# Elementwise work of norm rows, scans and combinations moved from GpSimd to VectorE in a four-layer mixed-attention forward pass

## The chip, the cores and the metric

One Trainium2 chip, one of its cores. The time is the device time of one execution of the whole forward pass in microseconds. The engines of the core are TensorE (PE in the profile; its weight loads are PEld), VectorE (DVE), ScalarE (ACT), GpSimd (POOL) and SyncE (SP, which issues most DMA transfers). Each executes its own list of instructions in order and waits for the others by semaphores.

## The reference

512 latent tokens and 256 context tokens, 1024 channels. Two blocks of two layers follow each other. In the first block, each layer is a norm with modulation by a condition (a gain and an offset per channel, different for latent and context tokens), two mixers side by side, a projection, a second such norm and an MLP. Layer 0 mixes by differential attention and a recurrent delta rule; layer 1 by two scans that run forwards and backwards, a state space scan (SSD, in chunks of 128) and a gated linear attention (GLA, here worked out in levels of halving blocks).

```python
def rmsnorm(x, g, eps=EPS):
    y = xf * lax.rsqrt(jnp.mean(xf * xf, axis=-1, keepdims=True) + eps)
    return (y * g.astype(F32)).astype(x.dtype)
...
        h = rmsnorm_2(x, norm1[l])
        proj = h @ w_in[l]
        o_a = dilated_mixture(...)
        o_b = stick_breaking_attention(...)
        merged = g_a * (o_a @ w_br[l, :OUT_A]) + g_b * (o_b @ w_br[l, OUT_A:])
        x = x + merged @ w_o[l]
        h2 = rmsnorm_2(x, norm2[l])
        up = h2 @ w_up[l]
        a = causal_depthwise_conv(a, conv_w[l], conv_b[l])
        x = x + (jax.nn.gelu(a, approximate=False) * v) @ w_down[l]
```

The second part of this is a layer of the second block: a mixture of windowed attentions of three dilations, each with its own softmax, that are combined by their maxima and denominators; a stick-breaking attention with a running sum of log-sigmoids; gates, projection, norm, and a gated MLP with a short convolution.

## The kernel before, in words

Channels lie on the 128 partitions and tokens along the free axis. Every large product is done in three passes of reduced-precision float32: an operand is split in a high half, which is its rounded copy, and a low half, which is what the rounding left; high by high, high by low and low by high are summed in PSUM. So each strip of weights (128 x 1024) that a DMA brings (`raw`, two buffers) goes through `_split` (L525): ScalarE casts it to `whi`, and then `wlo` = `raw` - `whi` is taken. By default VectorE takes it; while the flag `lazy` is set, GpSimd does. `layer1` sets the flag around the run of its mixers (L1748 to L1750).

The order of the work is made by a planner in the kernel (`Plan`, cost table at L300, `run` at L403). Stages are written as generators. `run` advances the one whose inputs are ready soonest by the planner's own costs of each engine; generators of the lowest priority (`FILL`) yield columns of a projection and go where nothing else is ready. Each instruction is recorded as it is yielded, and its order on its engine is fixed from then on. A changed engine of an instruction changes these costs and so the order of later instructions. All instructions go through one recording method (`Lane.call`, L245), so the profile tells them by the tiles that they write and read, not by lines.

What the change touches:

- `ada` (L768): the norm rows. For each of 8 channel groups, VectorE multiplies a piece by 1/rms (`t`), ScalarE makes the high half `H` of gain * t + offset, GpSimd makes the same in full (`u`, a `t` in the profile, L783), and VectorE subtracts. It runs at the second norm of layer 0 (two pieces of 384 tokens, 846 to 893 us), at the first norm of layer 1 (pieces of 512 and 256, up to 1463 us) and at the second norm of layer 1 (two pieces of 256, 1827 to 1857 us): 56 scalings.
- Layer 1's mixers (1446 to 1790 us). `layer1` (L1584) runs `fill()` (columns of the input projection, at the end the GLA's part of the output projection), `second()` (the GLA) and `first()` (the SSD). In `ssd_mix` (L1808) a step transposes decays into PSUM, ScalarE takes the exponential `E`, GpSimd multiplies it by C (`cT`, L1836), VectorE adds a mask (`G<-m,neg`), ScalarE takes the exponential of each head and VectorE multiplies by dt and C.B (`G<-G,sdt,cb`). In `gla_levels` (L1906) a level makes factors `QF` and `KF` from differences of cumulated decays (VectorE), their exponentials (ScalarE) and products with q and k (L1950, L1951; GpSimd for QF, and for KF of odd head pairs). `gla_prep` (L1896) has two differences on GpSimd, `gla_carry` (L2007) the product `qe`, `gla_post` (L2085) the output gate `yg` * `gs`. The convolution of the SSD (`t<-t,cw,t`, `bb`) is on VectorE in the same stretch.
- `block2` (L2141): in `dil` (L2355, L2359) the denominators' products and sums of the three dilations, once for each half of the heads and each layer; in `sb` (L2415) the running sums.

```python
        self.nc.scalar.copy(hi, raw)
        (self.nc.gpsimd if self.lazy else self.nc.vector).tensor_tensor(lo, raw, hi.bitcast(F32), op=SUB)
...
            nc.gpsimd.tensor_tensor(QF, QF, qT[:, t, :], op=MUL)
            (nc.gpsimd if t else nc.vector).tensor_tensor(KF, KF, kl[:, t, :], op=MUL)
```

## Time and profile before

| | before |
|---|---|
| median of 3 runs (lowest to highest) | 3707.17 us (3707.15 to 3709.8) |
| profiled execution, its span | 3708.26 us, 3706.5 us |
| mean granted TensorE clock | 0.983 |
| busy: PE, PEld | 3533.2 us (95%), 2935.0 us (79%) |
| busy: DVE, ACT, POOL | 2088.9 us (56%), 1540.0 us (42%), 641.9 us (17%) |
| instructions: PE, DVE, ACT, POOL | 25118, 3733, 2992, 817 |

Busy time is a mean over stages whose limits differ; the stretches are told apart by cutting the span into windows. The engine names in the rows are PE, PEld, DVE, ACT, POOL and SP. In a row of instructions, `out<-in` names the tile written and those read, then come partitions x elements and types of both, the count, busy time, mean time of one in ns, and the idle time of the engine before them with what ended it. Buffer numbers are left out, so several tiles share a name.

### The profile page before, as it was taken

To read this page: it belongs to the slowest core of one execution; us is meant where nothing else is said; L and a number is where in the kernel's file an instruction comes from. 1 tells how busy PE (TensorE), PEld (TensorE's weight loads), DVE (VectorE), ACT (ScalarE), POOL (GpSimd) and SP (SyncE) were. 2 spreads that over 40 slices of the span, in tenths; PEclk is the share of its full clock that TensorE was granted. 3 is DMA by queue.
4 is the path that set the end of the run, shared out by engine and by line. 5 is a ranking of instruction groups with operands and counts; after the bars stand their busy time and mean duration, and the time that the engine had idled before them with its cause. 6 is when DMAs were issued, how large, how long until landed. Compare 5 with 4: busy or idle time off the path is not lost.

```text
span 3706.5 us, 61484 instructions
## 1 busy us (share of the span) xinstructions
PE 3533.2 (95%) x25118; PEld 2935.0 (79%) x25118; DVE 2088.9 (56%) x3733; ACT 1540.0 (42%) x2992; POOL 641.9 (17%) x817
## 2 busy tenths in 40 slices
PE   7998998999999998888899999999999999999998
PEld 5786787888999997776788877777888777778886
DVE  5636787865433346588654465655554356555542
ACT  5424666634212224344532244555333245544331
POOL 3314233202000002443300020003110000031100
PEclk9999999999999999989999999999999999999999
DMA  5423311123333312110222232223333322232332
GB/s 207 114 82 130 126 50 38 32 89 114 109 125 111 117 63 88 52 41 24 97 96 97 98 120 71 63 74 109 97 97 101 124 68 63 74 103 94 97 95 90
DMA packets 128346, 337.10 MB, mean 91 GB/s; under 512 B 41536, under 2 KB 44608, under 8 KB 126912
## 3 DMA queue, kind: packets, MB, share of 16 engines
q1 hardware_dynamic: 113168, 297.31, 25.1%
q10 hardware_dynamic: 12432, 27.47, 2.3%
q0 software_dynamic: 2464, 8.39, 0.6%
q8 instruction: 198, 3.24, 0.4%
q14 instruction: 84, 0.69, 0.1%
HBM read 315.30 MB, written 17.83 MB: 90 GB/s over the span
## 4 chain that ended last, share of the span: by engine, by line
PE 67%; DVE 8%; ACT 2%; POOL 1%; issue 1%; DVEq 0%; POOLq 0%; ACTq 0%
PE g L245 61%; PE m L245 6%; DVE t L245 3%; POOL t L245 1%; DVE wlo L245 1%; PE pmod L245 1%; DVE G L245 1%; DVE QF L245 0%; DVE X L245 0%; ACT t L245 0%; DVE pk L245 0%; ACT pk L245 0%; ACT whi L245 0%; DVE KF L245 0%; DVE yg L245 0%
## 5 line engine op out<-in xcount | busy, mean ns | idle before, releaser
L245 PE MATMUL g<-pk,whi 128*128 128x512 f32 x3328 | 1081.1, 397 | 9.1 <-DVE t L245 4.2
L245 ACT CAST whi<-raw 128x1024 fp32r<-128x1024 f32 (+1 forms) x441 | 460.1, 1043 | 1242.8 <-PE g L245 1163.3
L245 PE MATMUL g<-H,whi 128*128 128x512 f32 (+2 forms) x2976 | 744.3, 358 | 21.1 <-ACT H L245 10.6
L245 DVE TENSOR_TENSOR wlo<-raw,whi 128x1024 fp32r<-128x1024 f32 (+1 forms) x414 | 508.6, 1228 | 432.9 <-ACT whi L245 424.5
L245 PEld LDWEIGHTS g<-pk,whi 128*128 128x128 f32 x3328 | 622.1, 189 | 148.0 <-issue 11.0
L245 PE MATMUL g<-pk,wlo 128*128 128x512 f32 x1824 | 717.5, 393 | 2.0 <-DVE wlo L245 2.0
L245 PEld LDWEIGHTS g<-H,whi 128*128 128x128 f32 x2976 | 515.2, 192 | 100.7 <-ACT H L245 13.4
L245 PE MATMUL g<-H,wlo 128*128 128x512 f32 (+2 forms) x1488 | 439.6, 353 | 11.3 <-POOL wlo L245 7.3
L245 PEld LDWEIGHTS g<-pk,wlo 128*128 128x128 f32 x1824 | 344.8, 189 | 76.8 <-DVE wlo L245 2.8
L245 PEld LDWEIGHTS g<-H,wlo 128*128 128x128 f32 x1488 | 261.3, 192 | 42.8 <-POOL wlo L245 8.9
L245 DVE SCALAR_TENSOR_TENSOR X<-g,mod,X 128x128 f32<-128x128 f32 (+3 forms) x320 | 162.8, 545 | 225.6 <-PE g L245 225.5
L245 PE MATMUL g<-hidh,whi 128*128 128x384 f32 (+2 forms) x896 | 276.1, 349 | 2.2 <-ACT hidh L245 1.3
L245 PE MATMUL g<-hidh,wlo 128*128 128x384 f32 (+2 forms) x896 | 275.0, 348 | 1.8 <-DVE wlo L245 1.7
L245 PE MATMUL g<-hidl,whi 128*128 128x384 f32 (+2 forms) x896 | 274.8, 347 | 0.2 <-DVE hidl L245 0.2
L245 PEld LDWEIGHTS g<-hidh,whi 128*128 128x128 f32 x896 | 165.6, 189 | 19.6 <-issue 6.7
L245 POOL TENSOR_TENSOR t<-t,t 128x512 f32<-128x512 f32 (+3 forms) x60 | 77.5, 1298 | 592.4 <-ACT t L245 301.6
L245 POOL TENSOR_SCALAR t<-t,gain,mod 128x256 f32<-128x256 f32 (+3 forms) x56 | 54.1, 974 | 725.4 <-DVE t L245 724.8
L245 PEld LDWEIGHTS g<-hidh,wlo 128*128 128x128 f32 x896 | 165.7, 189 | 13.5 <-DVE wlo L245 2.2
L245 PEld LDWEIGHTS g<-hidl,whi 128*128 128x128 f32 x896 | 166.0, 189 | 12.1 <-DVE hidl L245 0.5
L245 POOL TENSOR_TENSOR ssk<-ssk,t 128x512 f32<-128x512 f32 x37 | 64.7, 1762 | 574.8 <-ACT t L245 574.8
L245 ACT ACTIVATE t<-t 128x512 f32<-128x512 f32 (+5 forms) x179 | 98.5, 555 | 158.1 <-DVE t L245 156.1
L245 POOL TENSOR_TENSOR t<-t,rs 128x512 f32<-128x512 f32 x44 | 56.9, 1294 | 427.2 <-ACT t L245 427.2
(422 smaller groups left out, 5178.9 us busy)
## 6 DMA issues: line engine op xcount, KB each, us to landing
raw<-in_win_dram SPq DMA_DIRECT2D x131, 512.0 KB, 3.6
raw<-in_w_dram SPq DMA_DIRECT2D x130, 512.0 KB, 3.3
raw<-in_wup_dram SPq DMA_DIRECT2D x88, 512.0 KB, 3.6
mraw<-in_modw_dram SPq DMA_DIRECT2D x48, 512.0 KB, 5.7
raw<-in_modw_dram SPq DMA_DIRECT2D x32, 512.0 KB, 4.1
raw<-in_wda_dram SPq DMA_DIRECT2D x32, 512.0 KB, 3.6
room<-rkv ACTq DMA_DIRECT2D x48, 320.0 KB, 3.1
raw<-in_wout_dram SPq DMA_DIRECT2D x20, 512.0 KB, 3.3
```

What stands on the lines that cost most here:

```text
L245: r = f(*a, **k)
```

## The change

The flag `lazy` goes, and VectorE takes over 178 instructions: 27 low halves of weights, 56 scalings in `ada`, 16 `E` products, 2 differences in `gla_prep`, 14 QF and 7 KF products, 8 `qe`, 4 `yg` * `gs`, 12 products and 8 sums in `dil`, and 24 sums in `sb`. GpSimd keeps memsets, DMA issues, layer 0's work, sums of squares (`ssk`) and products of the second block's rotations.

```diff
-        (self.nc.gpsimd if self.lazy else self.nc.vector).tensor_tensor(lo, raw, hi.bitcast(F32), op=SUB)
+        self.nc.vector.tensor_tensor(lo, raw, hi.bitcast(F32), op=SUB)
...
-                    nc.gpsimd.tensor_scalar(u[:, at], t[:, at], gain[:, k, j : j + 1], mod[:, sh + k, j : j + 1], op0=MUL, op1=ADD)
+                    nc.vector.tensor_scalar(u[:, at], t[:, at], gain[:, k, j : j + 1], mod[:, sh + k, j : j + 1], op0=MUL, op1=ADD)
...
-            self.lazy = True
             self.run((fill(), FILL), second(), first(), late.stream(lambda: "zs" in done))
-            self.lazy = False
...
-                    nc.gpsimd.tensor_tensor(E, E, cT[:, g : g + 1, i0 : i0 + P].to_broadcast([P, 4, P]), op=MUL)
+                    nc.vector.tensor_tensor(E, E, cT[:, g : g + 1, i0 : i0 + P].to_broadcast([P, 4, P]), op=MUL)
...
-                (nc.gpsimd if t else nc.vector).tensor_tensor(x, x, o, op=SUB)
+                nc.vector.tensor_tensor(x, x, o, op=SUB)
...
-            nc.gpsimd.tensor_tensor(QF, QF, qT[:, t, :], op=MUL)
-            (nc.gpsimd if t else nc.vector).tensor_tensor(KF, KF, kl[:, t, :], op=MUL)
+            nc.vector.tensor_tensor(QF, QF, qT[:, t, :], op=MUL)
+            nc.vector.tensor_tensor(KF, KF, kl[:, t, :], op=MUL)
...
-                    nc.gpsimd.tensor_tensor(qe, qe, qT[:, :, ls], op=MUL)
+                    nc.vector.tensor_tensor(qe, qe, qT[:, :, ls], op=MUL)
...
-                nc.gpsimd.tensor_tensor(y, y, gs[:, h, :], op=MUL)
+                nc.vector.tensor_tensor(y, y, gs[:, h, :], op=MUL)
...
-                    nc.gpsimd.tensor_tensor(d, d, m, op=MUL)
+                    nc.vector.tensor_tensor(d, d, m, op=MUL)
...
-                        (nc.vector if n == 1 else nc.gpsimd).tensor_tensor(parts[0][n], parts[0][n], parts[r][n], op=ADD)
+                        nc.vector.tensor_tensor(parts[0][n], parts[0][n], parts[r][n], op=ADD)
...
-                            nc.gpsimd.tensor_tensor(sp[b][:, P:], sp[b][:, P:], sp[b + 1], op=ADD)
+                            nc.vector.tensor_tensor(sp[b][:, P:], sp[b][:, P:], sp[b + 1], op=ADD)
```

VectorE's list at the norm rows behind layer 0's mixers, as a piece of the difference (`t` the normed piece and its scaling, `gain` and `mod` the modulation, `X` the residual stream, `g` a projection's sum in PSUM, `H` the low half):

```order
+L245 TENSOR_SCALAR t_12421<-t_12420,gain_12181,mod_84 128x128
+L245 TENSOR_SCALAR t_12421<-t_12420,gain_12181,mod_84 128x256
+L245 SCALAR_TENSOR_TENSOR X_11790<-g_12407,mod_84,X_11790 128x384
 L245 TENSOR_TENSOR H_12186<-t_12421,H_12184 128x384
-L245 SCALAR_TENSOR_TENSOR X_11790<-g_12407,mod_84,X_11790 128x384
 L245 SCALAR_TENSOR_TENSOR X_11790<-g_12432,mod_84,X_11790 128x384
 L245 TENSOR_TENSOR t_12445<-X_11789,t_12377 128x384
```


The two scalings of a piece (context and latent tokens) now stand on VectorE between the product `t` and the difference `H`, and ahead of the residual's update from PSUM.

VectorE's list in the GLA's levels before (`cum` the cumulated decays, `t<-t,cw,t` and `bb` the SSD's convolution, `ke` a factor of the carried state):

```order
L245 TENSOR_TENSOR QF_17999<-cum_17247 128x16x16
L245 SCALAR_TENSOR_TENSOR t_17968<-t_17962,cw,t_17968 128x772
L245 TENSOR_TENSOR KF_17998<-cum_17247 128x16x16
L245 TENSOR_TENSOR QF_17999<-cum_17247 128x16x16
L245 TENSOR_TENSOR KF_17998<-cum_17247 128x16x16
L245 TENSOR_TENSOR QF_18058<-cum_17247 128x16x16
L245 TENSOR_TENSOR KF_18057<-cum_17247 128x16x16
L245 TENSOR_TENSOR QF_18058<-cum_17247 128x16x16
L245 SCALAR_TENSOR_TENSOR bb_17251<-t_17962,t_17968 128x512
L245 SCALAR_TENSOR_TENSOR bb_17251<-t_17962,t_17968 128x256
L245 TENSOR_TENSOR KF_18057<-cum_17247 128x16x16
L245 TENSOR_TENSOR KF_17998<-KF_17998,kT 128x512
```


The same place of the levels in the changed program:

```order
L245 TENSOR_TENSOR QF_18038<-QF_18038,qT 128x512
L245 TENSOR_TENSOR KF_18037<-KF_18037,kT 128x512
L245 TENSOR_TENSOR QF_18131<-cum_17247 128x16x16
L245 TENSOR_TENSOR KF_18130<-cum_17247 128x16x16
L245 TENSOR_TENSOR wlo_18115<-raw_17910,whi_18114 128x1024
L245 TENSOR_TENSOR QF_18131<-cum_17247 128x16x16
L245 TENSOR_TENSOR KF_18130<-cum_17247 128x16x16
L245 SCALAR_TENSOR_TENSOR t_18103<-t_18097,cw,t_18103 128x772
L245 TENSOR_TENSOR QF_18046<-QF_18046,qT 128x512
L245 SCALAR_TENSOR_TENSOR t_18103<-t_18097,cw,t_18103 128x772
L245 TENSOR_TENSOR KF_18045<-KF_18045,kT 128x512
L245 SCALAR_TENSOR_TENSOR t_18103<-t_18097,cw,t_18103 128x772
```


The products QF by q and KF by k, and the low half of a weight strip, now stand in line with the differences and the convolution; before, the products of QF and the low halves were in GpSimd's list.

VectorE's list at the last steps of the SSD before (`neg` the mask, `sdt` dt, `cb` C.B, `zs` and `gs` the gates, `ys` and `yg` the outputs):

```order
L245 TENSOR_TENSOR G_19940<-m_19899,neg 128x512
L245 TENSOR_TENSOR G_19979<-m_19911,neg 128x512
L245 SCALAR_TENSOR_TENSOR zs_19805<-t_19919,zs_19805 128x512
L245 SCALAR_TENSOR_TENSOR G_19940<-G_19940,sdt,cb 128x128 x4
L245 SCALAR_TENSOR_TENSOR G_19979<-G_19979,sdt,cb 128x128 x2
L245 TENSOR_TENSOR ys<-ys,zs_19805 128x512
```


And in the changed program:

```order
L245 SCALAR_TENSOR_TENSOR yg<-yg,cv,t_19915 128x512
L245 TENSOR_TENSOR yg<-yg,gs_19517 128x512
L245 SCALAR_TENSOR_TENSOR yg<-yg,cv,t_19916 128x512
L245 TENSOR_TENSOR E_19936<-E_19936,cT 128x512
L245 TENSOR_TENSOR yg<-yg,gs_19517 128x512
L245 TENSOR_TENSOR E_19947<-E_19947,cT 128x512
L245 TENSOR_TENSOR wlo_19960<-raw_19821,whi_19959 128x1024
L245 TENSOR_TENSOR G_19972<-m_19931,neg 128x512
L245 SCALAR_TENSOR_TENSOR zs_19811<-t_19954,zs_19811 128x512
L245 SCALAR_TENSOR_TENSOR G_19972<-G_19972,sdt,cb 128x128
L245 TENSOR_TENSOR G_19985<-m_19942,neg 128x512
L245 SCALAR_TENSOR_TENSOR G_19972<-G_19972,sdt,cb 128x128 x3
```


Two products of E, two of the gate and a low half now stand ahead of the sums and products of G.

## Rows read from the trace of the kernel before

**Rows 1.** The chain of waits that ended last, by engine
```profile
PE 67%; DVE 8%; ACT 2%; POOL 1%; issue 1%; DVEq 0%; POOLq 0%; ACTq 0%
```

**Rows 2.** Windows: length, busy of PE, PEld, DVE, ACT, POOL; clock, DMA share, GB/s
```profile
845.00:893.00 48.00, 42.69 (x213) 33.74 (x211) 33.06 (x58) 26.66 (x48) 21.25 (x24) 0.96 0.33 114
...
1420.00:1446.00 26.00, 16.78 (x109) 15.22 (x107) 18.96 (x33) 13.56 (x21) 9.29 (x7) 0.87 0.33 108
...
1446.00:1548.00 102.00, 96.24 (x632) 80.29 (x634) 51.74 (x115) 39.29 (x61) 40.03 (x28) 0.97 0.19 58
...
1548.00:1612.00 64.00, 49.64 (x480) 40.44 (x475) 63.65 (x90) 30.89 (x52) 36.52 (x32) 0.84 0.12 34
...
1660.00:1790.00 130.00, 109.45 (x709) 80.22 (x707) 107.50 (x213) 69.33 (x163) 50.58 (x35) 0.91 0.13 43
...
1811.00:1860.00 49.00, 43.11 (x299) 40.49 (x299) 33.23 (x70) 25.69 (x47) 17.29 (x16) 0.90 0.23 77
```

**Rows 3.** VectorE by form: four of 1548 to 1612, two of 1660 to 1790
```profile
L245 DVE TENSOR_TENSOR QF<-cum 128x256 f32<-128x256 f32 x20 | 18.0, 899 | 0.0
...
L245 DVE SCALAR_TENSOR_TENSOR t<-t,cw,t 128x772 f32<-128x772 f32 x12 | 17.8, 1480 | 0.1
...
L245 DVE TENSOR_TENSOR KF<-cum 128x256 f32<-128x256 f32 x19 | 10.0, 525 | 0.0
...
L245 DVE TENSOR_TENSOR KF<-KF,kT 128x512 f32<-128x512 f32 x4 | 5.4, 1342 | 0.1
...
L245 DVE SCALAR_TENSOR_TENSOR G<-G,sdt,cb 128x128 f32<-128x128 f32 x64 | 35.6, 609 | 1.0 <-ACT G L245 1.0
...
L245 DVE TENSOR_TENSOR G<-m,neg 128x512 f32<-128x512 f32 x16 | 10.5, 682 | 0.6 <-ACT E L245 0.5
```

**Rows 4.** Timeline: start, length, engine, instruction, idle before with its releaser
```profile
1547.61 2.52 POOL L245 TENSOR_TENSOR wlo<-raw,whi 128x1024 fp32r<-128x1024 f32 x1 [8.11 <-ACT whi L245]
...
1548.09 2.31 DVE L245 TENSOR_TENSOR QF<-cum 128x256 f32<-128x256 f32 x1
1550.33 0.41 DVE L245 TENSOR_TENSOR KF<-cum 128x256 f32<-128x256 f32 x1
...
1581.12 1.01 DVE L245 SCALAR_TENSOR_TENSOR t<-t,cw,t 128x772 f32<-128x772 f32 x1
...
1753.65 1.13 DVE L245 SCALAR_TENSOR_TENSOR G<-G,sdt,cb 128x128 f32<-128x128 f32 x4
...
1768.37 7.63 DVE L245 SCALAR_TENSOR_TENSOR G<-G,sdt,cb 128x128 f32<-128x128 f32 x6
...
1769.55 2.39 POOL L245 TENSOR_TENSOR wlo<-raw,whi 128x1024 fp32r<-128x1024 f32 x1
```

**Rows 5.** GpSimd by form, 1446 to 1790
```profile
L245 POOL TENSOR_TENSOR wlo<-raw,whi 128x1024 fp32r<-128x1024 f32 x24 | 58.2, 2425 | 79.5 <-ACT whi L245 68.2 <-PE m L245 8.4 <-ACT KF L245 2.9
```

**Rows 6.** TensorE's waits, 1446 to 1548 and 1660 to 1790: us in total, times, longest
```profile
PE g L245 <- POOL wlo L245: 4.5, 3, 2.1
...
PE m L245 <- DVE G L245: 10.3, 8, 2.4
...
PE g L245 <- POOL wlo L245: 2.8, 1, 2.8
```

**Rows 7.** VectorE: a wait of the whole span, and a form
```profile
DVE H L245 <- POOL t L245: 27.7, 44, 1.5
...
L245 DVE TENSOR_SCALAR kk<-kk 128x768 f32<-128x768 f32 x4 | 2.2, 561 | 12.4 <-ACT kk L245 12.4
```

**Rows 8.** First combination of the dilated attention: a wait of TensorE; VectorE by form, 2270 to 2303
```profile
2298.99 0.72 PE L245 MATMUL m<-ident,t 128*128 128x128 f32 x4 [2.59 <-DVE t L245]
...
L245 DVE TENSOR_TENSOR t<-t,t 128x512 f32<-128x512 f32 x10 | 10.8, 1117 | 0.1
```

**Rows 9.** Low halves on VectorE by form, 2200 to 2540 and 893 to 1420
```profile
L245 DVE TENSOR_TENSOR wlo<-raw,whi 128x1024 fp32r<-128x1024 f32 x45 | 56.3, 1252 | 7.3 <-ACT whi L245 3.7 <-PE g L245 3.5
...
L245 DVE TENSOR_TENSOR wlo<-raw,whi 128x1024 fp32r<-128x1024 f32 x61 | 74.4, 1220 | 156.7 <-ACT whi L245 156.7
```

More of the change, by code (lines that the diff above doesn't have):

```diff
@@ L1746, in first @@
                 yield from self.ssd_post(ys, gate["zs"], os_, one)
-            self.lazy = True
             self.run((fill(), FILL), second(), first(), late.stream(lambda: "zs" in done))
-            self.lazy = False
         with ExitStack() as es:
```

## The prediction, made before the changed kernel was run

> **What bounds the kernel now.** I read the chain of waits first [rows 1]: TensorE carries 67% of the span on it, VectorE 8%, ScalarE 2% and GpSimd 1%. TensorE's own matmuls are not touched by the change, so only places where TensorE stands still can pay. I then cut the span into stretches and took from each its length less TensorE's busy time [rows 2]: 48.00 - 42.69 = 5.3 us at layer 0's norm rows, 9.2 at the boundary to layer 1, 5.8, 14.4 and 20.6 in three stretches of layer 1's mixers, 5.9 at layer 1's norm rows, together 61 us. In the middle stretch of the mixers (1548 to 1612) VectorE is busy 63.65 of 64 us: there it is the bound, and not TensorE. Between 1660 and 1790 it is busy 107.50 of 130. The change gives VectorE 178 instructions more, so at first sight it loads the engine that is full.
>
> The groups by form say why VectorE is full [rows 3]. `QF<-cum` of 128x256 takes 899 ns in the mean, while one of the same size in the timeline takes 0.41 us; the convolution's `t<-t,cw,t` takes 1480 against 1.01; `G<-G,sdt,cb` 609 against 1.13 / 4 = 0.28 [rows 3, 4]. The timeline shows when it is long: the 2.31 us of `QF<-cum` begin under a GpSimd `wlo` that runs from 1547.61 for 2.52 us, and end as it ends; the next instruction, with GpSimd free, takes 0.41. Six `G` products take 7.63 us from 1768.37, over GpSimd's `wlo` at 1769.55. `G<-m,neg`, which reads one operand from PSUM, takes 682 ns for twice the columns and is not stretched. I read this as: a VectorE instruction with two operands in SBUF stands while a GpSimd product runs.
>
> The Trainium skill, "SBUF — State Buffer", section "Who interferes with whom", has VectorE's second pair of ports and GpSimd's only pair as one, held exclusively; the trace agrees with 2.31 us against 0.41.
>
> **The change part by part.** The trace of before is one execution of 3708.3 us, 1.1 above the median of the runs, 3707.2. The sum is of differences and is taken off the median. A measurement here can tell about 0.2% from no change, that is 7.4 us: faster means under 3699.8, slower over 3714.6.
>
> *Saturated stretch, 1548 to 1612.* Removed, if GpSimd is silent: QF (899 - 410) x 20 = 9.8 us, `t` (1480 - 1010) x 12 = 5.6, KF (525 - 410) x 19 = 2.2, KF's product with kT (1342 - 682) x 4 = 2.6: 20.2 us [rows 3, 4]. Added, by the instructions of this stretch: 9 QF and 5 KF products at 0.68 = 9.5 (the price of `G<-m,neg`, the nearest 128x512 row), 5 `wlo` at 1.22 [rows 9] = 6.1, 2 `qe` at 0.41 = 0.8: 16.4. VectorE does 3.8 us less, and as it is the bound there, TensorE gets them: **-4**. Ends: -14 (all of TensorE's idle time there), and +16 if nothing were given back.
>
> The Trainium skill, "Perfetto Trace Analysis", section "Optimizing Scalar/DVE Operations", says of a saturated VectorE that handing work to ScalarE or even to GpSimd may make sense, and adds that between VectorE and GpSimd it might not help because they share a port. Its first half speaks against this change and would make this term +16.4 in place of -4.
>
> *Low halves of weights in the mixers.* 24 `wlo` leave GpSimd, where one takes 2425 ns [rows 5], for VectorE, where it takes 1.22 us [rows 9]. TensorE waits 4.5 us in three places of 1446 to 1548 for GpSimd's `wlo`, and 2.8 once later [rows 6]: 7.3. Each of the four is shorter by 2.43 - 1.22 = 1.2 at best, **-4** taken; ends 0 and -7.3. But a `wlo` waits for ScalarE's cast `whi`. On GpSimd that wait (68.2 us in all [rows 5]) held back little; on VectorE whatever is queued behind stands too: the QF, KF, G and convolution steps, and through them TensorE's products. Where casts run early, VectorE loses 3.7 + 3.5 us for 45 `wlo`, 0.16 each; where it has little else to do, 156.7 for 61, 2.57 each [rows 9]. In the mixers VectorE is mostly behind ScalarE, so I take the first: 24 x 0.16 = **+4**; the second is a rival below.
>
> *Decay products and gates, 1660 to 1790.* Added: 16 E and 4 `yg` at 0.68, 7 `wlo` at 1.22, 6 `qe` at 0.41 = 24.6. Removed: G (609 - 283) x 64 = 20.9 [rows 3, 4], and some on forms not listed. VectorE's load stays about level, below the stretch's length. What TensorE waits for here is G, 10.3 us in 8 places [rows 6], a serial chain of sum, exponential and product in which the product becomes twice as fast; against that E's product now stands in line between G's. I take a third of the 17.8 us that TensorE idles in this stretch besides `wlo` (20.6 less 2.8): **-6**; ends -17 and +5 (a lone 128x512 in each of 8 waits). The mixers are then -4 - 4 + 4 - 6 = **-10**.
>
> *Norm rows.* 56 scalings go to VectorE. VectorE waits 27.7 us in 44 places, 0.63 each, for GpSimd's `t` before the difference H [rows 7]; a tensor_scalar of 128x768 takes 561 ns there [rows 7], and one of 256 columns between 0.28 (the 128x128 row [rows 4]) and that. So the scaling fills about what was waited for. TensorE idles 5.3 and 5.9 us at the two tails [rows 2]; I take a third of each, **-4** together; ends 0 and -11. At the boundary TensorE's 9.2 us stay as they are: they hang on the first H, and 8 more scalings on VectorE weigh up what GpSimd's wait gave. Ends -6 and +4.5 (8 x 0.56): 0.
>
> *Second block.* In each of the four combinations of the dilated attention 3 products and 2 sums move: 5 x 0.68 = 3.4 us more on VectorE, and its own ten `t<-t,t` fall from 1117 to about 690 ns: 4.3 less [rows 8]. GpSimd's serial run of five no longer ends last. TensorE waits 2.59 us there [rows 8], and as much in the other three: 4 x 1 = **-4**; ends 0 and -10.7. The 24 sums of the stick-breaking attention (at most 24 x 0.68 = 16 us over 1500) are hidden: TensorE does not wait for VectorE's or GpSimd's work there in any row that I found; cover gone, 16 us. 0.
>
> **Sum:** -10 - 4 - 4 = -18, **3689 us**.
>
> **The rivals.**
>
> *More is freed.* The stages feed each other, and a GpSimd that is silent lets two thirds of the 61 us go: 41, **3666 us**. For: 63.65 of 64 us on VectorE is a queue, and a queue's end moves by more than its mean. Against: what ScalarE's casts and exponentials hold up does not shrink with it.
>
> *Given back later.* The columns that fill TensorE while the mixers run are the same number; a planner puts them in by its own costs of engines, and these do not know that a GpSimd product stops VectorE. If the columns go sooner, the last steps of the scan run uncovered and the 14 us of the mixers come back as waits, while the standing stays: 3707 - 8 + 4 = **3703 us**.
>
> *VectorE stays saturated.* The stretched durations are not GpSimd's doing and do not shrink; then the 16.4 us lengthen the stretch: 3689 + 16 + 4 = **3709 us**. This is what the first half of the rule on saturation would have. Against: the 0.41 us right behind the 2.31.
>
> *Slower: VectorE stands for casts.* VectorE executes in order; a `wlo` put ahead of ready work waits for ScalarE's cast, 2.57 us each as in the layer 0 MLP [rows 9]: 24 x 2.57 = 62 us, of which what falls in the stretches where VectorE is nearly full counts, (64 + 130) / 344 = 0.56 of the mixers: +35. All gains (4 + 4 + 6 + 4 + 4 = 22) taken off: +13, **3720 us**. It decides from about 2.57 x 22 / 35 = 1.6 us per `wlo`. For: on GpSimd the wait was 68.2 / 24 = 2.8 us each, so casts come late there, or GpSimd early. Against: in 2200 to 2540, with VectorE as laden, it was 0.16.
>
> That the change does not do what it says is excluded: the changed program has 178 instructions more on VectorE and none of these on GpSimd.
>
> **How the numbers follow.** Forecast 0.65; more freed 0.05; given back 0.11; still saturated 0.03; standing for casts 0.16. Faster is the first two, **0.70**; same is the next two, **0.14**; slower **0.16**. The range's low end is the bigger gain, 3666; its high end is the forecast with every gain at zero and the standing left, 3707 + 4 = 3711. It holds all but the slower case: somewhat over 8 in 10 by these chances, and I leave it there because the planner's new order (the order of most later instructions shifts) may add a few us either way.
>
> **What would show it.** Right: VectorE's busy time falls although it has 178 instructions more; `QF<-cum` near 0.41, `t<-t,cw,t` near 1.0, G near 0.3; the idle of TensorE in 1548 to 1612 under 11 us; the combinations' waits of 2.6 us under 2. Wrong: the durations of these forms stay (then the stretching was not GpSimd's); or VectorE's idle before `wlo` in the mixers, put down to `whi`, is over 1.6 us each while TensorE waits for G, QF or `bb`; or waits in the mixers shrink and TensorE's idle before the last projection grows by as much.

## The result and the profile after

The changed kernel takes 3665.08 us (median of 4 runs, 3662.96 to 3666.98) against 3707.93 us of the kernel before in the same series: ratio 0.9884, 95% interval 0.9866 to 0.9901. That is 43 us, where 18 were forecast; the measured time lies a microsecond under the range (3666 to 3711), at the price of the rival "more is freed". The direction was right and the size was not. The profiled execution's span is 3661.2 us, 45.3 less than before, at a mean granted clock of 0.989 (0.983 before).

Totals and chain of the changed kernel: VectorE has 178 instructions more and is busy 2097.5 us, 8.6 more than before, not the some 115 that they cost by themselves after (27 low halves at 1.22, 56 scalings of 24 us in all, 61 products and sums of 128x512 at 0.69, and 15 us of smaller ones). TensorE executes as many matmuls as before in 17.5 us less busy time.

```profile
PE 3515.7 (96%) x25118; PEld 2924.1 (80%) x25118; DVE 2097.5 (57%) x3911; ACT 1539.5 (42%) x2992; POOL 394.1 (11%) x639
...
PE 72%; DVE 4%; ACT 1%; issue 1%; DMA 0%; POOL 0%; DVEq 0%; ACTq 0%; POOLq 0%
```

VectorE by form, first one row of the mixers before (1446 to 1790), then the mixers after (1447 to 1757), against [rows 3]: the stretched forms are at the prices of free ones.

```profile
L245 DVE TENSOR_TENSOR QF<-cum 128x256 f32<-128x256 f32 x28 | 21.3, 760 | 0.0
```

```profile
L245 DVE TENSOR_TENSOR wlo<-raw,whi 128x1024 fp32r<-128x1024 f32 x26 | 31.7, 1221 | 7.3 <-ACT whi L245 7.2
L245 DVE SCALAR_TENSOR_TENSOR t<-t,cw,t 128x772 f32<-128x772 f32 x24 | 24.4, 1018 | 0.2 <-ACT t L245 0.2
L245 DVE SCALAR_TENSOR_TENSOR G<-G,sdt,cb 128x128 f32<-128x128 f32 x64 | 18.6, 348 | 1.3 <-ACT G L245 1.2
L245 DVE TENSOR_TENSOR QF<-cum 128x256 f32<-128x256 f32 x28 | 11.8, 421 | 0.0
...
L245 DVE TENSOR_TENSOR G<-m,neg 128x512 f32<-128x512 f32 x16 | 10.6, 684 | 0.0
```

`QF<-cum` went from 899 ns in the saturated stretch, and 760 over all the mixers, to 421, `t<-t,cw,t` from 1480 in that stretch to 1018, G from 609 to 348; `G<-m,neg`, with an operand in PSUM, is where it was (682, now 684). VectorE stands 7.3 us before 26 `wlo`, waiting for casts, 0.28 each: the rival of 2.57 each did not come.

**Where the time came from.** I lined the two traces up by the n-th matmul of the projections, of which both have 13,190. Until the mixers begin, the changed kernel is 1.2 us behind: it is 2.0 ahead at the end of layer 0's mixers, where nothing was changed (so 2 us in this lining up can be chance), and loses 0.9 at layer 0's norm rows and 2.4 at the boundary. Over the mixers and the output projection behind them (to 1811 us) it gains 34.4, at layer 1's second norm 1.3, and in the second block's two layers 3.6 and 7.2. The sum is -45.2, the difference of the spans.

The windows of the mixers, before and then after (length; busy of PE, PEld, DVE, ACT, POOL; clock):

```profile
1446.00:1790.00 344.00, 297.07 (x2117) 236.17 (x2117) 255.98 (x462) 163.47 (x313) 142.00 (x109) 0.92 0.15 47
```

```profile
1447.00:1754.00 307.00, 284.55 (x2110) 229.34 (x2111) 243.06 (x538) 160.41 (x308) 3.00 (x24) 0.95 0.17 54
```

VectorE takes over nearly all the work of GpSimd's 142 us and is still busy 13 us less. TensorE idles 22.5 in place of 46.9 us, and its almost equal number of matmuls takes 12.5 us less: the granted clock of the stage is 0.95 in place of 0.92 (297.07 x 0.92 / 0.95 = 287.7, so by estimate some 9 of the 12.5). The prediction had no term for that.

The saturated stretch, cut in both traces from the 5,146th to the 5,315th matmul of the projections:

```profile
1550.00:1609.00 59.00, 45.75 (x422) 37.58 (x421) 58.65 (x86) 28.26 (x48) 32.52 (x32) 0.83 0.13 37
```

```profile
1544.00:1583.00 39.00, 37.98 (x382) 31.80 (x381) 36.30 (x65) 21.93 (x37) 0.64 (x11) 1.00 0.17 55
```

59 us became 39: 12.2 us are TensorE's idle time and the rest is 45.75 - 37.98 = 7.8 of busy time, for 40 matmuls fewer (small ones of the levels, which moved behind) and at a clock of 1.00 in place of 0.83. Part of this is work that moved behind the stretch: the lead is 27.1 us at 1612 us of the trace before, and 16.6 at 1664, as the levels are finished later; from 1548 to 1664 it grows by 12.4. The largest single wait in the stretch was one of 6.4 us for `bb`, the end of a convolution. TensorE's waits of all the mixers, before, then after:

```profile
PE m L245 <- DVE bb L245: 10.4, 2, 6.4
PE m L245 <- DVE G L245: 10.3, 8, 2.4
PE g L245 <- POOL wlo L245: 7.3, 4, 2.8
...
PE m L245 <- POOL KF L245: 2.6, 2, 2.2
```

```profile
PE g L245 <- DVE wlo L245: 5.9, 3, 3.5
PE m L245 <- DVE G L245: 5.4, 3, 3.0
...
PE m L245 <- DVE bb L245: 0.5, 1, 0.5
```

Before, TensorE waits for GpSimd itself only 7.3 + 2.6 = 9.9 us of the 46.9 that it idles in the mixers.

### The profile page after: what moved, and what is told of

It is laid out like the page before. It is cut to its first block, busy times and chain, and to the rows that moved or that the text cites. A ratio compares the mean times of both kernels' runs of the same rounds, so it can differ in the third digit from the quotient of the medians.

```text
span 3661.2 us, 61339 instructions
## 1 busy us (share of the span) xinstructions
PE 3515.7 (96%) x25118; PEld 2924.1 (80%) x25118; DVE 2097.5 (57%) x3911; ACT 1539.5 (42%) x2992; POOL 394.1 (11%) x639
## 4 chain that ended last, share of the span: by engine, by line
PE 72%; DVE 4%; ACT 1%; issue 1%; DMA 0%; POOL 0%; DVEq 0%; ACTq 0%; POOLq 0%
PE g L245 65%; PE m L245 6%; DVE t L245 1%; DVE wlo L245 1%; PE pmod L245 1%; DVE X L245 0%; ACT whi L245 0%; ACT t L245 0%; DVE KF L245 0%; DVE QF L245 0%; POOL t L245 0%; DVE H L245 0%; DVE cum L245 0%; ACT pk L245 0%; ACT cum L245 0%
## 5 line engine op out<-in xcount | busy, mean ns | idle before, releaser
L245 PE MATMUL g<-pk,whi 128*128 128x512 f32 x3328 | 1074.2, 396 | 10.4 <-DVE t L245 5.5
L245 DVE TENSOR_TENSOR wlo<-raw,whi 128x1024 fp32r<-128x1024 f32 (+1 forms) x441 | 538.8, 1222 | 444.8 <-ACT whi L245 435.3
L245 DVE TENSOR_TENSOR t<-g,rs 128x512 f32<-128x512 f32 x64 | 47.5, 742 | 142.8 <-PE g L245 140.9
L245 ACT COPY t<-m 128x512 f32<-128x512 f32 (+3 forms) x220 | 97.8, 481 | 74.2 <-PE m L245 73.6
L245 PE MATMUL g<-hl,whi 128*128 128x512 f32 x320 | 126.3, 395 | 0.0
```

Of the source, the lines that this page charges most:

```text
L245: r = f(*a, **k)
```

## The experiments

The theory: a VectorE instruction with two operands in SBUF stands while a GpSimd product runs (called the hold from here on); a silent GpSimd gives VectorE its own speed back, and TensorE part of its idle time and of its clock. Rival A: GpSimd was only slow in handing results on. Rival B: VectorE's queue stands for casts. Rival C: the planner's new order did it, since moved instructions change the planner's costs and so the order of all later work.

**Parts put back in the changed kernel.** e1: the flag `lazy` again around the mixers. e2: the products of the mixers again on GpSimd.

```diff
-        self.nc.vector.tensor_tensor(lo, raw, hi.bitcast(F32), op=SUB)
+        (self.nc.gpsimd if self.lazy else self.nc.vector).tensor_tensor(lo, raw, hi.bitcast(F32), op=SUB)
```

> The changed kernel, with the 24 to 27 low halves of weights of layer 1's mixers back on GpSimd; everything else stays on VectorE. Theory of the hold (a VectorE instruction with two operands in SBUF stands while a GpSimd product runs): about 58 us of GpSimd products come back in the mixers, and before the change 142 us of GpSimd went with some 68 us of stretched VectorE work; so some 28 us of stretch come back, while VectorE is relieved of 24 x 1.22 = 29 us: 3664 to 3680. Rival A, that GpSimd was only slow in handing results on: TensorE's waits for low halves go from 5.9 to about 7.3 us and nothing else: 3665 to 3668. Rival B, that VectorE's queue now stands for the casts: faster than the changed kernel, 3655 to 3662.

3669.90 us, 4.8 over the changed kernel and inside the theory's range; rival A's ends 1.9 us below it, which these runs do not tell apart. Rival B is out (it would have been faster). In the trace `t<-t,cw,t` is at 1254 ns again, from 1018.

```diff
-                    nc.vector.tensor_tensor(E, E, cT[:, g : g + 1, i0 : i0 + P].to_broadcast([P, 4, P]), op=MUL)
+                    nc.gpsimd.tensor_tensor(E, E, cT[:, g : g + 1, i0 : i0 + P].to_broadcast([P, 4, P]), op=MUL)
...
-            nc.vector.tensor_tensor(QF, QF, qT[:, t, :], op=MUL)
+            nc.gpsimd.tensor_tensor(QF, QF, qT[:, t, :], op=MUL)
```

> The changed kernel, with the products of the mixers (E, QF, KF of odd head pairs, qe, the output gate and two differences of the preparation: 51 instructions, some 76 us of GpSimd) back on GpSimd, and the low halves left on VectorE. Theory of the hold: some 36 us of stretch come back where VectorE is nearly full and 35 us of its work leave it; what is left is the handing over and TensorE's clock: 3675 to 3692. Rival A (only slow handing on): the products lie in serial chains and each takes 0.7 to 1.1 us longer: 3680 to 3695, with QF<-cum and G staying at their short times. Rival C (the planner's order did it): no number of its own here, but the short times stay.

3672.19 us, 7.1 more: under both ranges. `QF<-cum` went to 521 ns and G to 429, between the two kernels. Each part alone costs little; two more runs below (f3, f4) take that up in another order.

**The order of before with the new engines (e3).** The planner is told that the 178 instructions run on GpSimd; they run on VectorE.

```diff
+        self.booked = Lane(nc.vector, "pool", self)
...
-            nc.vector.tensor_tensor(QF, QF, qT[:, t, :], op=MUL)
+            nc.booked.tensor_tensor(QF, QF, qT[:, t, :], op=MUL)
```

> The changed kernel's engines, but the planner books the 178 moved instructions on GpSimd as before, so the order of the work stays nearly that of the kernel before. Theory of the hold: the gain comes from the silent GpSimd and not from the order; most of it stays, 3662 to 3680. Rival C (the new order made the gain): most of it goes, 3690 to 3712.

3651.59 us, ratio 0.9852 (0.9838 to 0.9867): 13.5 us faster than the changed kernel. Rival C is wrong, and the other way round: the new order cost time, and the engines alone bring 56 us. (The order is nearly that of before: by the traces 226 of TensorE's 25,118 instructions stand elsewhere, 666 in the changed kernel.) The planner's better knowledge of where an instruction runs made a worse order. Nor can rival A make most of this: over the mixers e3 gains 39 us on the kernel before, lined up, and TensorE's waits for GpSimd there were 9.9.

**Products that nobody waits for (e4).** Of VectorE's instructions five stand elsewhere than in the changed kernel, of TensorE's 26.

```diff
+                    nc.scalar.eng.copy(tick, pp[0][0][:, :1])
+                    g.tensor_tensor(idle[:, :1], tick, tick, op=MUL)
+                    for _ in range(13):
+                        g.tensor_tensor(idle, self.ident, self.ident, op=MUL)
```

> The changed kernel, with GpSimd products added in layer 1's mixers that nobody waits for: behind each of 23 columns, 14 products of 128x128 or less on a constant, some 140 us in all, as much GpSimd work as before the change; the order of all other work stays. Theory of the hold: VectorE's instructions with two SBUF operands stretch again (QF<-cum from 0.42 towards 0.6 to 0.9 us, the convolution's from 1.02 towards 1.3), VectorE's busy time in the mixers rises by 40 to 70 us from 243, and as that stage has only some 60 us of room, the time is 3685 to 3715. Rival A and rival C: nobody waits for these products and no order changes: 3664 to 3668, durations unchanged.

3697.07 us (10 runs, 3691.09 to 3700.65): 32 of the 43 us are gone, though nobody reads what these products make. VectorE by form in the mixers, then GpSimd:

```profile
L245 DVE TENSOR_TENSOR wlo<-raw,whi 128x1024 fp32r<-128x1024 f32 x27 | 35.1, 1305 | 6.5 <-ACT whi L245 6.5
...
L245 DVE TENSOR_TENSOR QF<-cum 128x256 f32<-128x256 f32 x28 | 14.4, 514 | 0.0
...
L245 DVE TENSOR_TENSOR G<-m,neg 128x512 f32<-128x512 f32 x16 | 10.6, 682 | 0.0
```

```profile
L1620 POOL TENSOR_TENSOR idle<-ident 128x128 f32<-128x128 f32 x279 | 167.0, 599 | 21.7
```

The forms with two SBUF operands stretch (421 to 514, 1221 to 1305), the one with a PSUM operand does not (682). From 1489 to 1515 VectorE has no gap, its list is the same as in the changed kernel, and e4 falls 7.2 us behind there; a window of that, and two waits of ScalarE in the mixers:

```profile
1489.00:1515.00 26.00, 17.38 (x86) 14.23 (x85) 26.00 (x51) 9.34 (x17) 19.20 (x40) 0.94 0.21 61
```

```profile
ACT t L245 <- POOL t L245: 10.1, 2, 6.1
...
ACT hidh L245 <- POOL idle L1620: 7.1, 1, 7.1
```

So the hold is shown: rivals A and C allow no stretch. But the 32 us are not all of it. GpSimd still sets the borders of the convolution's tiles to zero (24 memsets in the mixers), and in e4 these stand in its queue behind the idle products: ScalarE waits 10.1 us for two of them, and at the end 7.1 us for the last idle products. In the profiled execution, lined up, e4 loses 36 us on the changed kernel over the mixers, and 18 of them at these two places (14.0 and 4.1). Nor is the rest a share of the gain: in e4 VectorE keeps the moved instructions, and the dose is another than before (176.7 us of products with the triggering ones, in 344, against 142, in smaller pieces that stretch less each). How much of the mixers' gain the hold makes is not measured; what speaks for most of it is that handing on has 9.9 us to give.

**One part at a time, in e3's order.** Base is e3 at 3651.6 us; only the engine of one part is changed. The planner's costs are the same in all, yet the lists in the traces are not quite: 32, 148 and 173 of TensorE's instructions stand elsewhere in f1, f3 and f4, one at most in f2, g1 and g2; of VectorE's 32 in f1, 55 in f3, 82 in f4, and 20 in f2 and g2, all at the combinations. So "fixed from then on", as the description of the planner has it, does not hold for VectorE's list. In each, `nc.booked` of the part becomes `nc.gpsimd`, for f2:

```diff
-                    nc.booked.tensor_tensor(d, d, m, op=MUL)
+                    nc.gpsimd.tensor_tensor(d, d, m, op=MUL)
...
-                            nc.booked.tensor_tensor(sp[b][:, P:], sp[b][:, P:], sp[b + 1], op=ADD)
+                            nc.gpsimd.tensor_tensor(sp[b][:, P:], sp[b][:, P:], sp[b + 1], op=ADD)
```

> From the kernel with the order of before and the new engines (e3_order_of_before, 3651.6 us), the 56 scalings of the norm rows run on GpSimd again, in the same order. By the term of the prediction (a third of TensorE's idle time at the norm rows): 3656. Rival, from the traces of the changed kernels, where TensorE's wait at the boundary to layer 1 went from 6.4 to 8.0 and 9.6 us: the scalings gained nothing or lost 2 to 4 us on VectorE: 3647 to 3652.

> From the kernel with the order of before and the new engines (3651.6 us), the 12 products and 20 to 32 sums of the second block's two attentions run on GpSimd again, in the same order. By the term of the prediction (4 combinations of 1 us): 3656. By what the traces show after the second block's mixers (20 us between the order-of-before kernel and before): 3668 to 3672.

> From the kernel with the order of before and the new engines (3651.6 us), the low halves of layer 1's mixers run on GpSimd again, in the same order. Theory of the hold: the stretch of 60 to 75 us of GpSimd products against 30 us of relief on VectorE, and it costs less than its share of the 36 us, because one part alone leaves VectorE room in the stage: 3656 to 3666. Rival A (only slow handing on): 24 casts to low halves are 1.2 us longer, a few of them waited for: 3653 to 3657.

> From the kernel with the order of before and the new engines (3651.6 us), the 53 products and differences of layer 1's mixers run on GpSimd again, in the same order. Theory of the hold: 3658 to 3672, with QF<-cum near 0.55 us and G near 0.43 as when they were put back with the new order. If the parts simply added, this and the low halves would together cost the 36 us that the mixers gained; theory: clearly less than 36 together, since either part alone leaves VectorE below its stage's length.

> From the kernel with the order of before and the new engines (3651.6 us), the sums of the stick-breaking attentions alone run on GpSimd again, in the same order. The prediction put them at 0, and the traces show TensorE's new waits only at the four combinations of the dilated attention: 3651 to 3654. Rival (the sums stretch VectorE and hold up the stick-breaking chain): 3658 to 3664.

> From the kernel with the order of before and the new engines (3651.6 us), the 12 products and 8 sums of the combinations alone run on GpSimd again, in the same order. By the term of the prediction (1 us in each of 4 places): 3656. By the traces (at each of the 4 places 2.6 to 4.5 us of TensorE's idle time, and as much again of slower matmuls behind it): 3668 to 3672.

| put back on GpSimd | us | ratio to before, 95% | against e3 |
|---|---|---|---|
| f1 scalings of the norm rows | 3648.88 | 0.9843 (0.9828 to 0.9857) | -2.7 |
| f3 low halves in the mixers | 3660.04 | 0.9872 (0.9857 to 0.9887) | +8.4 |
| f4 products in the mixers | 3659.13 | 0.9871 (0.9854 to 0.9887) | +7.5 |
| f2 second block, both attentions | 3672.14 | 0.9905 (0.9890 to 0.9920) | +20.5 |
| g1 its stick-breaking sums | 3648.47 | 0.9840 (0.9825 to 0.9855) | -3.1 |
| g2 its combinations | 3670.62 | 0.9900 (0.9884 to 0.9917) | +19.0 |

f1 and g1 are within the interval of e3: the scalings and the sums bring nothing that these runs can tell. The four combinations bring 19 us. The low halves and the products of the mixers cost 16 us together when put back one by one, against the 39 that the mixers of e3 gain on before by the lined-up traces. The likely reason, which no run separates: with one part alone on GpSimd, VectorE still has room in the stage, with both it has not.

At the first combination with its work back on GpSimd (g2), the timeline (start, length, engine, instruction):

```profile
2248.01 8.89 POOL L245 TENSOR_TENSOR t<-t,t 128x512 f32<-128x512 f32 x5 [65.39 <-ACT t L245]
...
2252.27 5.17 DVE L245 TENSOR_TENSOR t<-t,t 128x512 f32<-128x512 f32 x3
...
2257.37 0.94 DVE L245 RECIPROCAL t<-t 128x128 f32<-128x128 f32 x1
...
2258.77 0.67 DVE L245 TENSOR_TENSOR t<-g,rs 128x512 f32<-128x512 f32 x1
...
2259.50 0.66 PE L245 MATMUL m<-ident,t 128*128 128x128 f32 x4 [2.62 <-DVE t L245]
```

Three of VectorE's `t<-t,t` take 1.72 us each under GpSimd's five. TensorE waits for `t<-g,rs`, which stands behind them in VectorE's list. In e3 VectorE does fifteen such in the stretch, at 686 ns:

```profile
L245 DVE TENSOR_TENSOR t<-t,t 128x512 f32<-128x512 f32 x15 | 9.5, 686 | 0.2
```

What a wait costs beyond itself is seen in the windows of the kernel before at the same place, the wait and the 6 us behind it:

```profile
2296.00:2299.00 3.00, 0.41 (x3) 0.02 (x1) 3.00 (x5) 0.00 (x0) 0.38 (x1) 1.00 0.00 0
2299.00:2305.00 6.00, 6.00 (x22) 4.87 (x23) 4.72 (x9) 1.68 (x3) 0.00 (x0) 0.72 0.30 87
```

TensorE waits 2.59 us [rows 8], and then works 6 us at a mean granted clock of 0.72 (a mix of 1.2 and 2.4 GHz), where about 6 x 0.28 = 1.7 us more are lost. Lined up over the second block, e3 gains 20.4 us on f2, 13.4 of idle time and 7.0 of slower matmuls, nearly all of it at and behind the four combinations.

**Idle products at the combinations.** Is it the hold there too, or GpSimd's serial run of five ending last? The trace of g2 answers the second half. In all four places VectorE works without a gap until TensorE goes on, and GpSimd's run ends 0.5 to 1.1 us before VectorE comes to its first reciprocal (2256.90 against 2257.37 above). From 2200 to 3200 VectorE's waits for GpSimd's tiles are the same in e3 and in g2:

```profile
DVE t L245 <- POOL t L245: 46.7, 22, 2.1
```

For the first half, i1 and i2 take e3 with products on a constant beside each combination, triggered by its maximum; the order of all other work is unchanged. i2 has 7 of 128x320 in place of 14 of 128x128.

```diff
                 nc.vector.tensor_tensor(M, M, parts[2][0], op=MAX)
+                idle = self.small([P, P], "idle", 1)
+                g.tensor_tensor(idle[:, :1], M[:, :1], M[:, :1], op=MUL)
+                for _ in range(14):
+                    g.tensor_tensor(idle, self.ident, self.ident, op=MUL)
```

> From the kernel with the order of before and the new engines (3651.6 us), at each of the four combinations of the dilated attention GpSimd gets 14 small products on a constant that nobody waits for, some 8.5 us, as long as its five products and sums took there before. Theory of the hold: VectorE's t<-t,t of the combination stretch from 0.69 us towards 1.1 and TensorE waits again; VectorE keeps the five more instructions, so it is at least as late as with them on GpSimd: 3660 to 3675. Rival A (the gain was GpSimd's slow serial run of five, not the hold): 3650 to 3654.

> As i1_idle_at_combinations (3652.1 us, in which 15 t<-t,t went from 0.69 to 0.82 us in the mean), but with 7 products of 128x320 in place of 14 of 128x128, some 8 us that nobody waits for: if small products hold VectorE for a smaller part of their length, these hold it more, as the five of 128x512 did that ran beside three t<-t,t of 5.17 us. Theory of the hold at the combinations: t<-t,t near 1.0 us and TensorE waiting at all four: 3656 to 3672. Rival A (GpSimd's serial run of five): 3650 to 3654 again.

i1: 3652.14 us, no loss that the runs can tell, though VectorE's `t<-t,t` went from 686 to 819 ns and TensorE waits 2.4 us in two of the four places: a miss for the hold at this dose. i2: 3659.81 us (0.9872, 0.9856 to 0.9889), with TensorE waiting 6.6 us over the four places, where e3 has no such wait. VectorE by form at the first combination, then TensorE's waits for 2200 to 3200, both of i2:

```profile
L245 DVE TENSOR_TENSOR t<-t,t 128x512 f32<-128x512 f32 x14 | 12.0, 907 | 0.1
```

```profile
PE m L245 <- DVE t L245: 6.6, 4, 2.1
```

The cost rises steeply with the stretch: 819 ns costs nothing that the runs tell, 907 costs 8 us, and the 1117 of the real work goes with 19. In i2 the order is e3's, so its 8 us are the hold's. In g2 something else differs too: VectorE has five instructions less there, and in its list a reciprocal and a product stand ahead of the `t<-g,rs` that TensorE waits for (1.4 us at the first combination, 2257.37 to 2258.77), while in e3 they stand behind it. How the 19 divide between the longer stretch and this order stays open; at the first combination the stretch of ten `t<-t,t`, 10 x (1.117 - 0.686) = 4.3 us, is more than the whole wait of 2.6, the order is less.

**What the new order costs (h1).** The changed kernel, with only the second block's 44 instructions booked on GpSimd (running on VectorE).

> The changed kernel, but the planner books the 44 instructions of the second block's attentions on GpSimd as before, so there the order of before stays; layer 1 is as in the changed kernel. The traces put some 9 of the 13.5 us between the two orders into the second block: 3655 to 3658. Rival (the orders differ in their gain in layer 1): 3662 to 3666.

3652.81 us: 12.3 of the 13.5 us between the orders are in the second block. Lined up, the changed kernel loses most of them at the projections behind the second layer's mixers. TensorE at the same place of the first layer, in the changed kernel and then in h1 (timeline):

```profile
2471.05 2.37 PE L245 MATMUL m<-t,vb 128*64 128x512 f32 x8 [1.44 <-ACT t L245]
2475.27 0.96 PE L245 MATMUL g<-ot,whi 128*128 128x512 f32 x3 [1.86 <-ACT ot L245]
```

```profile
2466.83 2.37 PE L245 MATMUL m<-t,vb 128*64 128x512 f32 x8
2471.00 0.96 PE L245 MATMUL g<-ot,whi 128*128 128x512 f32 x3 [1.80 <-ACT ot L245]
```

In the new order the last product of the stick-breaking chain (`m<-t,vb`) waits for ScalarE with no column left to run beside it. In the second layer the same two waits of the changed kernel are 1.44 and 1.86 us (3210 and 3214), of which h1 has neither, and the granted clock from 3210 to 3220 is 0.83, in h1 1.00. Lined up, h1 gains 10.6 us on the changed kernel over the second block, 9.3 of them in the second layer, where TensorE idles 4.9 us less and is busy 4.4 less. How much of that the clock is, and how much the other places of columns, was not followed up.

**Going on.** b1: e3, and the second block's remaining elementwise products (`u` * `rs`, `t0` + `t1`) and the sums of squares on VectorE, booked on GpSimd. b2: layer 0's products too. best_mixed: b1, with the scalings of layer 0's second and layer 1's first norm back on GpSimd.

```diff
-                nc.gpsimd.tensor_tensor(u, u, rs, op=MUL)
+                nc.booked.tensor_tensor(u, u, rs, op=MUL)
...
-                    nc.booked.tensor_scalar(u[:, at], t[:, at], gain[:, k, j : j + 1], mod[:, sh + k, j : j + 1], op0=MUL, op1=ADD)
+                    (nc.booked if (l, sh) == (1, 24) else nc.gpsimd).tensor_scalar(u[:, at], t[:, at], gain[:, k, j : j + 1], mod[:, sh + k, j : j + 1], op0=MUL, op1=ADD)
```

> The kernel with the order of before and the new engines (3651.6 us), and besides the remaining elementwise products and sums of the second block, and the sums of squares, move from GpSimd to VectorE without a change of the order. Theory of the hold: 94 us of waits of VectorE for GpSimd's t and some 70 us of stretched VectorE work go there, but TensorE idles little in those stages (7 to 11 us in the whole second block): 3640 to 3650. Rival A (TensorE hides it): 3650 to 3653.

> As b1_more_moved, and layer 0's products too move from GpSimd to VectorE (192 small ones in its recurrence, its rotations and shifts), order as before. In layer 0's recurrence VectorE is busy 80 to 90% in places, with GpSimd 45 to 60%: theory of the hold: within 10 us of b1_more_moved, either way. Rival: VectorE gets 192 x 0.2 = 38 us more there and TensorE waits for it: 15 to 40 us slower than b1_more_moved.

> b1_more_moved (3642.8 us), with the scalings of layer 0's second norm and of layer 1's first norm on GpSimd, and those of layer 1's second norm left on VectorE. The traces put 0.6 and 3 us on the first two: 3637 to 3642. Rival (GpSimd's few products there stretch VectorE as they do elsewhere): 3643 to 3648.

b1: 3642.81 us (0.9830, 0.9814 to 0.9847), most of it behind the second layer's mixers. b2: 3647.33 (0.9840, 0.9825 to 0.9855), 4.5 over b1 and not told from it by the intervals; lined up, some 7 us go to layer 0, as VectorE is busy 387 of 475 us there without these products already. best_mixed: 3639.52 (0.9813, 0.9799 to 0.9828), the fastest kernel of the study, 26 us under the changed one; its 3.3 us on b1 are within the interval.

## Why the prediction was right or wrong, point by point

- **The reading of the bound was right.** VectorE was full in 1548 to 1612 because GpSimd's products stretched it. e4 shows the stretch with products that nobody needs, and every form named in the prediction fell to the price taken for it, G to 348 instead of 283.
- **The saturated stretch, -4, was mis-sized; lined up it measured -20, or -12 with what moved behind it, to 1664 us.** The step that failed is "VectorE does 3.8 us less, and as it is the bound there, TensorE gets them". It set all of the moved work of 64 us against the stretch only of the forms listed, and by "only places where TensorE stands still can pay" it took TensorE's own time as fixed. Measured: 12.2 us less idle time (the lower bound of -14 was nearer), and 7.8 of busy time less at a clock of 1.00 instead of 0.83. Part of the idle time was a wait for one late tile, `bb` (6.4 us in the stretch and 4.0 behind it, not in the sum): four convolution steps one after the other took 2.00, 1.72, 1.16 and 3.12 us where one takes 1.01, and a late tile moves by all of them.
- **TensorE's clock had no term.** The clock of the stretch, 0.84, stood in [rows 2] and was not used. Over the mixers it is worth, by the estimate above, some 9 of the 12.5 us by which TensorE's busy time fell; over the second block slower matmuls make 7.0 of f2's 20.4.
- **The low halves, -4, and their standing, +4.** Waits for `wlo` fell by 1.4 only, 7.3 to 5.9 [rows 6]; the standing is 0.28 us each, 7 us and not 4. Both small, as the prediction had it; the slower rival needed 1.6 each. The row set against that rival was misread: from 2200 to 2540 VectorE is busy 207 of 340 us, not "as laden" as in the mixers (256 of 344).
- **G and gates, -6.** TensorE's waits for G, `ke` and `yg` fell from 17.6 to 9.7 us: -7.9, right.
- **The mixers' sum, -10, measured -37 by the windows, -34 with the projection behind them.** The parts do not add: put back one by one they cost 8.4 and 7.5 us, together they gained 39 (e3, lined up).
- **The norm rows, -4, came out at about +2 with the boundary.** With the scalings back on GpSimd the time is the same (f1, -2.7, within the interval). Lined up, the two tails, put at -2 each, lose 0.9 us at layer 0 and gain 1.3 at layer 1. At the boundary, put at 0, TensorE's first wait grew from 6.4 to 9.6 us, and to 8.0 in e3, and 2.4 us are lost: in the changed kernel it ends with VectorE's update of `X`, which now stands behind the scalings in VectorE's list.
- **The combinations, -4, were mis-sized.** In e3's order they bring 19 us: lined up, 12.4 of idle time (the bound was put at 10.7; 4 x 2.59 is 10.4) and 6.3 of slower matmuls behind the waits. The changed kernel keeps some 11 us of gain in the second block. "GpSimd's serial run of five no longer ends last" was a misreading: before, the run ends at 2296.38, and VectorE comes to its first reciprocal at 2296.85 without a gap ahead of it. What ended last was VectorE's own list.
- **The sums of the stick-breaking attention, 0: right** (g1).
- **The rival "given back later" was half right in mechanism and wrong in place.** The new order gives 12 us back, in the second block and not in the mixers, most of it behind the last product of a chain.
- **The first half of the Trainium skill's rule on a saturated engine** ("Perfetto Trace Analysis", section "Optimizing Scalar/DVE Operations") would have lengthened the stretch by 16.4 us; it shrank by 20. The caveat in the same place, the port that GpSimd shares with VectorE, fits the stretch in e4; that a port is the reason is the page's word, no run here shows it.

## What to carry to other kernels

Before pricing work that moves from GpSimd to VectorE, compare the mean time of VectorE's forms with two SBUF operands with their shortest: what lies between may be GpSimd's doing, and a late engine's relief falls on the tile that is waited for, all at once, not on the mean. Waits of TensorE of 1 to 3 us in a busy stage cost here about half as much again in slower matmuls behind them (13.4 and 7.0 us in f2), so count the granted clock of the stretch in the sum. Idle products that nobody reads price the hold in place without a new order, but look first for what else stands in the queue behind them. Where a planner orders the work by its own costs, try the new engines with the old order too: here the better-informed order was worse by 13 us.

## What the runs showed of the hardware that was not expected

Small GpSimd products stretch VectorE less than large ones: in e4, 177 us of small ones in 344 raised the mean of `QF<-cum` over the mixers only from 421 to 514 ns, where the kernel before, with 142 us in larger pieces, had 760; and at the combinations 14 of 128x128 in 11.6 us cost nothing that the runs tell, 7 of 128x320 in 8.4 us cost 8 us over the four places. From 1505 to 1511 in e4 the small instructions of VectorE start every 0.54 us in place of 0.335, while GpSimd's products of 128x128 follow each other every 0.59: by this estimate each holds VectorE for some 0.2 us, a third of its time. The Trainium skill, "SBUF — State Buffer", section "Summary: rules for kernel authors", has the second of the two to issue blocked until the first finishes, where VectorE's instruction has two inputs in SBUF and GpSimd's reads SBUF. The large pieces here agree (2.31 us against 0.41 [rows 4]), the small ones do not; no run separates the size from the number of products.

GpSimd is slowed too: its `QF<-QF,qT` takes 2212 ns in e2, where VectorE makes the low halves, against 1743 in the kernel before, where GpSimd made them itself (the profile's spans of GpSimd are rough).
